# A running sum moved from GpSimd adds to accumulating DMAs, and 16 subtractions moved from GpSimd to VectorE

## The chip, the core and the metric

The kernel runs on one core of one Trainium2 chip. A core has five engines that run their own instruction streams in order and wait for each other through semaphores: TensorE (PE) multiplies matrices, VectorE (DVE) and ScalarE (ACT) work elementwise on SBUF and PSUM, GpSimd (POOL) works elementwise on SBUF, and SyncE (SP) issues DMAs; ACT and POOL issue DMAs too. The metric is the time of one execution on the device, in microseconds (us). A kernel is run several times and the median is given.

## The reference

The model is one layer of a residual block on a sequence of 1024 tokens with 1024 channels, in float32:

```
h = rms_norm(x) * (1 + sc1) + sh1
b, c, v, vc, gl, gates = split(h @ w_in)                    # seven groups of 1024 columns
y_a = (b * causal_dwconv(c * v, 3 taps)) @ w_short_out
u   = causal_dwconv(vc * sigmoid(gl), 31 taps) + bias
y_b = silu(layer_norm(u) over channels) @ w_conf_out
x   = x + g1 * ((sigmoid(ga) * y_a + sigmoid(gb) * y_b) @ w_o)
x   = x + g2 * swiglu_ffn(rms_norm(x) * (1 + sc2) + sh2)
out = rms_norm(x)
```

For the change, two things matter. `q = b * causal_dwconv(c * v, 3 taps)` is the operand of the projection to `y_a`. And LayerNorm needs, for each token, the mean of `u` over all 1024 channels.

## The kernel before

Activations lie with channels on the 128 partitions and tokens along the free dimension, so 1024 channels are eight tiles, numbered j, of 128 x 1024. Every matrix product is made from three fp32r products: an operand is split into a rounded part ("hi", a cast on ScalarE) and the rest ("lo", a subtraction), and PE adds hi·hi, hi·lo and lo·hi in PSUM (lines 283, 284 and 286). Weights are split the same way by `split_w` (lines 205 and 206) as they arrive; up to three blocks are prepared ahead of the one in use.

Most of the input projection, `h @ w_in`, is done by a seven-product scheme on 2 x 2 blocks. There are 12 "duals", each of them two column blocks and seven products, in the order of the string `PRODUCTS`. The weights of a product are sums of weight blocks: GpSimd makes these sums (lines 228 to 232) and the lo parts (line 206) for all 12 duals and for `w_short`; the instructions of its lo parts are collected in `pool_los`. PE results are taken out of PSUM by ScalarE copies and VectorE operations (`win_evac`, lines 551 to 615), which also form `u` before the convolution (kind "u"), the short convolution `sc[j]` (kind "p", line 538) and `q` (kind "q"). `q_store(j)` splits q into hi (ScalarE, line 529) and lo (GpSimd, line 530), and SyncE stores both in DRAM (line 532); `q_load` brings them back while the last dual runs (line 622).

Beside the duals runs the 31-tap convolution, `conv(j)` for the eight channel tiles: 46 VectorE multiply-adds into two PSUM tiles (line 647) for each, then ScalarE writes even and odd tokens back into u's own tile (line 660), and ScalarE's queue stores it as `cv_dram[j]` (line 661). `add_conv(j)` then adds that tile into `tot`, two SBUF tiles of 128 x 512 that hold the running sum over j (line 667). So `tot` ends as the sum over j for each partition; `ln_mean` (line 674) multiplies it with a matrix of ones on PE (line 678), which sums over partitions, and divides on ScalarE (line 679). `ln_square` loads cv back (line 687), subtracts the mean (line 689) and sums squares. All this takes place beside the eight column blocks of `ya`, the product of q with `w_short`; `ln_mean` stands behind the first of them in the program. The next product, `yb`, needs the normalised tiles (`zs`).

The order of the work on each engine is fixed when the kernel is built, by a planner that takes instructions in program order as priority and by its own estimate of when each is ready. `tc.issue_after(ins)` adds that an instruction comes behind `ins` on its engine: the taps are spread over the PSUM reads of the duals in that way, and `add_conv(j)` is put behind a certain weight lo part in GpSimd's queue. An instruction that waits holds up all behind it on its engine. The tiles of u, p, sc, q and the gates share eight buffers (pool "uc"), and the small 128 x 512 tiles share 58 (pool "t").

Of the kernel before, what the change touches and what calls it, by code (L numbers as in the profile page):

```python
# [34 lines left out]
F32 = mybir.dt.float32  # L35
F32R = mybir.dt.float32r
AF = mybir.ActivationFunctionType
ALU = mybir.AluOpType

P = 128  # L40
D = 1024
T = 1024
H = 512
# [64 lines left out]
def block_kernel(ctx: ExitStack, tc: tile.TileContext, x0, xT, c, vecs, ada, w_first, w_plain, w_duals,  # L108
                 w_short, w_conf, w_o, w_fi, w_fo, w_last, outT):
    nc = tc.nc  # L110

    def pool(name, bufs, **kw):
        return ctx.enter_context(tc.tile_pool(name=name, bufs=bufs, **kw))
# [18 lines left out]
    dram = pool("scratch", 1, space=bass.MemoryType.DRAM)  # L132
# [11 lines left out]
    def hl_tile(name, dt=F32R):  # L144
        return tp.tile([P, H], dt, tag="t", name=name)
# [7 lines left out]
    def f32(t):  # L153
        return t.bitcast(F32)

    halves = (slice(0, H), slice(H, T))
# [251 lines left out]
    u = []  # L408
    gate_dram = {(b, j): dram.tile([P, T], F32, name=f"gate_{b}{j}") for b in "ab" for j in range(KC)}

    def uc_tile(name, n=T + CK - 1, dt=F32):
        return ucp.tile([P, T + CK - 1], dt, tag="uc", name=name)[:, :n]
# [24 lines left out]
    for k in range(0, KC, 2):  # L437
        t = uc_tile("x0", T)
# [83 lines left out]
    sc = [None] * KC  # L522
    q_dram = {}

    def q_store(j):

        for h in range(2):
            s = uc_tile("qs", T, F32R)
            nc.scalar.copy(s[:, :H], sc[j][:, halves[h]])
            nc.gpsimd.tensor_tensor(s[:, H:], sc[j][:, halves[h]], f32(s[:, :H]), ALU.subtract)  # L530
            q_dram[j, h] = dram.tile([P, T], F32, name=f"q{j}{h}")
            nc.sync.dma_start(q_dram[j, h], f32(s))

# [17 lines left out]
    def win_evac(pairs):  # L551
# [15 lines left out]
        def evac(i, m, ps):  # L567
# [22 lines left out]
            elif m == "5":  # L590
                e["z"] = e["c"][1] if kind == "g" else g_tile("z")
                nc.scalar.copy(e["z"], ps)
            elif m == "7":
                plus(e["z"], ps, e["z"])
                if kind in "ug":
                    nc.scalar.activation(e["z"], e["z"], AF.Sigmoid, scale=-1.0)
                elif kind == "q":
                    minus_times(sc[j + 1][:, halves[1]], e["z"], sc[j + 1][:, halves[1]])
            else:
                if kind in "ug":  # L600
                    sig = e["c"][0] if kind == "g" else g_tile("sig")
                    nc.scalar.activation(sig, ps, AF.Sigmoid, scale=-1.0)
                if kind == "u":
                    nc.vector.tensor_tensor(e["b"][0], e["b"][0], sig, ALU.mult)
                elif kind == "p":
                    minus_times(e["b"][0], ps, e["b"][0])
                    short_conv(j, e["p"])
                elif kind == "q":
                    minus_times(sc[j + 1][:, halves[0]], ps, sc[j + 1][:, halves[0]])
                    for i in range(2):  # L610
                        q_store(j + i)
                else:
                    for g, t in zip((j, *rest), e["t"]):
                        nc.scalar.dma_start(gate_dram[g], t)
# [17 lines left out]
    def conv(j):  # L632
        eo = u[j].rearrange("p (n two) -> p n two", two=2)
        ev, od = eo[:, :, 0], eo[:, :, 1]
        diff = diffp.tile([P, T + CK - 1], F32, tag="diff", name="diff")
        d, e = diff[:, :NE], diff[:, NE : 2 * NE - 1]
        with tc.issue_after(reads[j * CONV_READS // KC]):
            nc.vector.tensor_tensor(d, ev, od, ALU.subtract)
            nc.vector.tensor_tensor(e, ev[:, 1:], od[:, : NE - 1], ALU.subtract)
        a0, a1 = ps2_tile("c0"), ps2_tile("c1")  # L640
        n = 0

        def tap(out, src, s, wt, acc):
            nonlocal n
            n += 1
            with tc.issue_after(reads[(j * TAPS + n) * CONV_READS // (KC * TAPS)]):
                tap.ins = nc.vector.scalar_tensor_tensor(  # L647
                    out=out, in0=src[:, s : s + H], scalar=wt, in1=acc, op0=ALU.mult, op1=ALU.add
                ).ins

        nc.scalar.activation(a0, od[:, :H], AF.Copy, scale=wsum[:, j : j + 1])
        for s in range(1, CK // 2 + 1):
            last = s == CK // 2
            tap(a0, od, s, col(V_CW + 2 * s * KC, j) if last else wsum[:, s * KC + j : s * KC + j + 1], a0)
        for s in range(CK // 2):
            tap(a1, e, s, col(V_CW + (2 * s + 1) * KC, j), a1 if s else a0)
        for s in range(CK // 2 + 1):
            tap(a0, d, s, col(V_CW + 2 * s * KC, j), a0)
        for i, a in enumerate((a0, a1)):
            nc.scalar.activation(eo[:, : H, i], a, AF.Identity, bias=col(V_CB, j))  # L660
        nc.scalar.dma_start(cv_dram[j], u[j][:, :T])

    def add_conv(j):

        with tc.issue_after(pool_los[(j + 1) * CONV_READS * 7 // (6 * KC) + 5]):
            for h in range(2):
                nc.gpsimd.tensor_tensor(tot[h], tot[h], u[j][:, halves[h]], ALU.add)

    cv = []
    tot = [hl_tile(f"tot{h}", dt=F32) for h in range(2)]  # L670
    for t in tot:
        nc.gpsimd.memset(t, 0.0)

    def ln_mean():
        mu = []
# [57 lines left out]
    for j in range(KC):  # L733
        conv(j)
        add_conv(j)
    ma = {}
    for j in range(KC):
        for h, ps in enumerate(col_block(next_w(), qT, (0, 1), "ya")):
# [424 lines left out]
```

## Time and profile before

| | |
|---|---|
| Median of 3 runs | 1522.57 us (1522.05 to 1522.73) |
| Profiled execution, its own time | 1522.49 us |
| Span of the profiled execution | 1520.7 us |
| Mean granted clock of PE | 0.991 |
| Busy: PE, VectorE, ScalarE, GpSimd | 1474.4, 1179.8, 612.5, 580.9 us |
| Work by GpSimd in line 667 (the sums) | 16 instructions |
| Work by GpSimd in line 530 (q's lo parts) | 16 instructions |

All numbers of the trace come from one execution; its span runs from the first to the last instruction. In the rows of groups, "out<-in" names the tiles written and read, x is the count, then come the busy time in us, the mean of one in ns, and the idle time of the engine just before these instructions with what ended it. In the rows of waits, "A <- B: total, times, longest" says how long A stood still until B released it. Rows of a timeline or of the chain of waits begin with the start and the duration in us. Engine names with a small q are the engine's queue.

### The profile page before, as it was taken

What the parts mean: (1) busy time and instruction counts of PE and PEld (TensorE: products, weight loads), DVE (VectorE), ACT (ScalarE), POOL (GpSimd) and SP (SyncE); (2) the same over time, 40 slices, a digit from 0 to 9 for tenths busy, and PEclk for the clock granted to TensorE, in tenths of its full rate; (3) what the DMA queues carried; (4) which work ended last, traced back from release to release, by engine and by line L of the source; (5) the groups of instructions that cost most, each with busy time, mean ns of one, the idle gap of its engine ahead of it and who ended that gap; (6) DMA issues with size and microseconds to landing.
All of it is one profiled execution on the core that took longest, in us unless ns stands there. A gap on an engine that the chain in (4) does not pass through costs nothing.

```text
span 1520.7 us, 17802 instructions
## 1 busy us (share of the span) xinstructions
PE 1474.4 (97%) x6449; PEld 1202.4 (79%) x6449; DVE 1179.8 (78%) x1566; ACT 612.5 (40%) x871; POOL 580.9 (38%) x483
## 2 busy tenths in 40 slices
PE   6999999999998999999999989999999999999996
PEld 2888887877886888878788868888888888788886
DVE  7997898999997972867777789776666665677756
ACT  4754343443333342335335454444444443211234
POOL 0037788798768883410021001111000016445005
PEclk9999999999999999999999989999999999999998
DMA  9522223232222269655765436554444449998403
GB/s 356 195 63 83 83 70 138 69 111 98 97 84 97 62 223 415 227 180 173 236 203 168 142 103 220 204 171 153 153 152 152 153 153 351 355 299 267 138 15 111
DMA packets 87306, 255.64 MB, mean 168 GB/s; under 512 B 10033, under 2 KB 12209, under 8 KB 87218
## 3 DMA queue, kind: packets, MB, share of 16 engines
q1 hardware_dynamic: 46384, 146.30, 28.7%
q0 software_dynamic: 36944, 95.44, 19.0%
q10 hardware_dynamic: 3890, 12.78, 2.1%
q8 instruction: 50, 0.82, 0.2%
q14 instruction: 38, 0.31, 0.1%
HBM read 187.89 MB, written 66.58 MB: 167 GB/s over the span
## 4 chain that ended last, share of the span: by engine, by line
PE 77%; DVE 10%; DMA 5%; POOL 3%; issue 3%; ACT 1%; SPq 0%; DVEq 0%; ACTq 0%; POOLq 0%
PE x L286 11%; PE x L283 11%; PE x L284 11%; PE z L283 6%; PE z L286 6%; PE z L284 6%; PE y L284 4%; PE y L283 4%; PE y L286 4%; DVE c L647 3%; DMA raw<-in_ada 2%; PE mix L283 2%; PE mix L284 2%; PE mix L286 2%; PE yb L284 2%
## 5 line engine op out<-in xcount | busy, mean ns | idle before, releaser
L205 ACT CAST wh<-raw 128x1024 fp32r<-128x1024 f32 (+2 forms) x257 | 259.0, 1009 | 412.9 <-PE z L284 102.9
L206 POOL TENSOR_TENSOR wl<-raw,wh 128x1024 fp32r<-128x1024 f32 x92 | 237.2, 2586 | 85.5 <-ACT wh L205 85.3
L206 DVE TENSOR_TENSOR wl<-raw,wh 128x1024 fp32r<-128x1024 f32 (+2 forms) x165 | 188.1, 1141 | 50.3 <-ACT wh L205 47.7
L647 DVE SCALAR_TENSOR_TENSOR c<-diff,vec,c 128x512 f32<-128x512 f32 x248 | 182.2, 749 | 6.4 <-DMA q<-qs 2.6
L910 POOL DMA_DIRECT2D hid<-stage x71 | 37.9, 534 | 359.6 <-DVE stage L323 353.3
L284 PE MATMUL x<-tl,wh 128*128 128x512 f32 x336 | 130.7, 389 | 0.0
L283 PE MATMUL x<-th,wh 128*128 128x512 f32 x336 | 130.7, 389 | 0.0
L286 PE MATMUL x<-th,wl 128*128 128x512 f32 x336 | 130.7, 389 | 0.0
L647 DVE SCALAR_TENSOR_TENSOR c<-u,wsum,c 128x512 f32<-128x512 f32 x112 | 84.0, 750 | 1.9
L286 PE MATMUL x<-t2h,wl 128*128 128x512 f32 x184 | 74.2, 404 | 6.2 <-POOL wl L206 5.1
L283 PE MATMUL x<-t2h,wh 128*128 128x512 f32 x184 | 73.5, 401 | 5.5 <-ACT wh L205 2.8
L264 DVE CUSTOM_DVE_ANT_0 raw<-raw,cs,vec 128x1024 f32<-128x1024 f32 x24 | 34.5, 1441 | 52.2 <-DMA raw<-in_ada 41.0
L283 PEld LDWEIGHTS x<-th,wh 128*128 128x128 f32 x336 | 63.1, 188 | 13.1 <-issue 0.2
L284 PE MATMUL x<-t2l,wh 128*128 128x512 f32 x184 | 73.3, 399 | 0.1
L284 PEld LDWEIGHTS x<-tl,wh 128*128 128x128 f32 x336 | 63.1, 188 | 13.1
L286 PEld LDWEIGHTS x<-th,wl 128*128 128x128 f32 x336 | 63.1, 188 | 13.1
L283 PE MATMUL z<-th,wh 128*128 128x512 f32 x168 | 65.4, 390 | 1.6 <-ACT wh L205 1.6
L228 POOL TENSOR_TENSOR raw<-raw 128x1024 f32<-128x1024 f32 x12 | 29.2, 2436 | 98.6 <-DVE wl L206 94.0
L286 PE MATMUL z<-th,wl 128*128 128x512 f32 x168 | 65.5, 390 | 0.0
L284 PE MATMUL z<-tl,wh 128*128 128x512 f32 x168 | 65.4, 389 | 0.0
L322 ACT CAST stage<-g 128x512 fp32r<-128x512 f32 x62 | 38.3, 621 | 55.7 <-DMA hid<-stage 27.8
L323 DVE TENSOR_TENSOR stage<-g,stage 128x512 fp32r<-128x512 f32 x62 | 42.4, 687 | 22.8 <-ACT stage L322 22.6
(797 smaller groups left out, 4081.6 us busy)
## 6 DMA issues: line engine op xcount, KB each, us to landing
hid<-stage POOLq DMA_DIRECT2D x71, 512.0 KB, 4.2
raw<-in_w_fi SPq DMA_DIRECT2D x50, 512.0 KB, 4.4
raw<-in_w_duals SPq DMA_DIRECT2D x48, 512.0 KB, 3.5
th<-hid POOLq DMA_DIRECT2D x71, 256.0 KB, 5.7
tl<-hid POOLq DMA_DIRECT2D x71, 256.0 KB, 6.2
ada<-in_ada SPq DMA_DIRECT2D x24, 512.0 KB, 6.2
raw<-in_ada SPq DMA_DIRECT2D x24, 512.0 KB, 4.6
raw<-in_w_fo SPq DMA_DIRECT2D x24, 384.0 KB, 5.9
```

The lines of the kernel that those rows point to most:

```text
L205: nc.scalar.copy(wh, raw)
L206: lo = lo_engine.tensor_tensor(wl, raw, f32(wh), ALU.subtract)
L228: eng.tensor_tensor(a["s1"], a["21"], a["22"], ALU.add)
L264: nc.vector.tensor_tensor_reduce(out=raw, in0=raw, in1=cs, scale=1.0, scalar=col(V_ADA, b), op0=ALU.mult, op1=ALU.add, accum_out=modc(b),)
L283: nc.tensor.matmul(ps, wh, xh, start=first, stop=False, skip_group_check=again)
L284: nc.tensor.matmul(ps, wh, xl, start=False, stop=False, skip_group_check=again)
L286: mm3.ins = nc.tensor.matmul(ps, wl, xh, start=False, stop=last, skip_group_check=again).ins
L322: nc.scalar.copy(hi, src)
L323: nc.vector.tensor_tensor(lo, src, f32(hi), ALU.subtract)
L647: tap.ins = nc.vector.scalar_tensor_tensor(out=out, in0=src[:, s : s + H], scalar=wt, in1=acc, op0=ALU.mult, op1=ALU.add).ins
L910: nc.gpsimd.dma_start(hid_dram[key], s)
```

## The change

Two things move off GpSimd's arithmetic. First, q's lo parts (line 530) are made by VectorE instead of GpSimd. Second, the running sum no longer lies in SBUF: `tot_dram` is a DRAM tile of 128 x 1024, and `add_conv(j)` issues one DMA from GpSimd's queue that stores u's tile there for j = 0 and adds it to what is there for the others, at the same place in GpSimd's order as the two adds before. The two SBUF tiles `tot` are allocated after the last `add_conv` and loaded from `tot_dram` by two DMAs, also from GpSimd's queue; the two memsets go. `ln_mean` is as before.

```diff
@@ -527,7 +527,7 @@
         for h in range(2):
             s = uc_tile("qs", T, F32R)
             nc.scalar.copy(s[:, :H], sc[j][:, halves[h]])
-            nc.gpsimd.tensor_tensor(s[:, H:], sc[j][:, halves[h]], f32(s[:, :H]), ALU.subtract)
+            nc.vector.tensor_tensor(s[:, H:], sc[j][:, halves[h]], f32(s[:, :H]), ALU.subtract)
             q_dram[j, h] = dram.tile([P, T], F32, name=f"q{j}{h}")
             nc.sync.dma_start(q_dram[j, h], f32(s))
 
@@ -663,13 +663,10 @@
     def add_conv(j):
 
         with tc.issue_after(pool_los[(j + 1) * CONV_READS * 7 // (6 * KC) + 5]):
-            for h in range(2):
-                nc.gpsimd.tensor_tensor(tot[h], tot[h], u[j][:, halves[h]], ALU.add)
+            nc.gpsimd.dma_start(tot_dram, u[j][:, :T], **({"accum_op": ALU.add} if j else {}))
 
     cv = []
-    tot = [hl_tile(f"tot{h}", dt=F32) for h in range(2)]
-    for t in tot:
-        nc.gpsimd.memset(t, 0.0)
+    tot_dram = dram.tile([P, T], F32, name="tot")
 
     def ln_mean():
         mu = []
@@ -733,6 +730,9 @@
     for j in range(KC):
         conv(j)
         add_conv(j)
+    tot = [hl_tile(f"tot{h}", dt=F32) for h in range(2)]
+    for t, s in zip(tot, halves):
+        nc.gpsimd.dma_start(t, tot_dram[:, s])
     ma = {}
     for j in range(KC):
         for h, ps in enumerate(col_block(next_w(), qT, (0, 1), "ya")):
```

## The prediction

> **What bounds the kernel now.** I read the page first, then the waits of PE, then the busy table by stretches.
>
> ```profile
> span 1520.7 us, 17802 instructions
> PE 1474.4 (97%) x6449; PEld 1202.4 (79%) x6449; DVE 1179.8 (78%) x1566; ACT 612.5 (40%) x871; POOL 580.9 (38%) x483
> ```
>
> PE is busy for 97% of the span, so a change pays only where it removes idle or slow PE time. POOL's 38% is an average that hides the stage in question, from about 96 to 584 us, where the seven-product input projection runs beside the convolution. There PE waited for this:
>
> ```profile
> PE x L286 <- POOL wl L206: 8.8, 5, 3.5
> PE x L283 <- ACT u L577: 0.4, 1, 0.4
> PE y L286 <- POOL wl L206: 0.4, 1, 0.4
> ```
>
> These are the waits of PE between 200 and 560 us (total, times, longest). Of 9.6 us, 9.2 are for POOL's low part of a weight block; none is for VectorE. The table by stretches (columns PE, PEld, DVE, ACT, POOL busy with instruction counts, PE clock, DMA share, GB/s) shows where:
>
> ```profile
> 290.00:310.00 20.00, 18.85 (x83) 15.28 (x83) 19.82 (x27) 8.12 (x10) 17.20 (x8) 1.00 0.23 80
> 350.00:370.00 20.00, 18.57 (x82) 15.04 (x81) 19.29 (x27) 8.93 (x13) 15.35 (x9) 1.00 0.48 159
> 410.00:430.00 20.00, 20.00 (x90) 16.57 (x89) 19.86 (x23) 7.45 (x9) 19.42 (x8) 1.00 0.03 2
> 450.00:470.00 20.00, 17.08 (x75) 13.52 (x74) 16.12 (x23) 8.00 (x11) 19.53 (x10) 1.00 0.13 53
> 470.00:490.00 20.00, 16.52 (x65) 13.13 (x65) 19.73 (x27) 4.35 (x6) 16.10 (x7) 0.91 0.41 131
> 200.00:560.00 360.00, 350.40 (x1527) 286.70 (x1527) 337.47 (x437) 134.49 (x183) 295.55 (x130) 1.00 0.30 100
> ```
>
> A full stretch holds 90 matmuls, 0.222 us each (third row). The other four 20 us rows hold 83, 82, 75 and 65: 55 missing, 55 x 0.222 = 12.2 us of PE. That is more than the waits, because PE comes back slow after the longest one: the granted clock of that stretch is 0.91, and the chain of waits shows matmuls of double length there.
>
> ```profile
> 479.55 0.24 PE x L283
> ...
> 480.40 0.43 PE x L283
> ```
>
> What POOL did before the waits, in order of time (start, duration):
>
> ```profile
> 292.56 3.47 POOL L667 TENSOR_TENSOR tot<-tot,u 128x512 f32<-128x512 f32 x2 [3.50 <-ACT u L660]
> ...
> 352.07 3.00 POOL L530 TENSOR_TENSOR qs<-sc,qs 128x512 fp32r<-128x512 f32 x2
> ...
> 452.68 1.75 POOL L667 TENSOR_TENSOR tot<-tot,u 128x512 f32<-128x512 f32 x1
> ...
> 456.75 1.29 POOL L667 TENSOR_TENSOR tot<-tot,u 128x512 f32<-128x512 f32 x1
> ...
> 466.10 1.30 POOL L530 TENSOR_TENSOR qs<-sc,qs 128x512 fp32r<-128x512 f32 x1
> ...
> 472.20 4.48 POOL L530 TENSOR_TENSOR qs<-sc,qs 128x512 fp32r<-128x512 f32 x2
> 476.65 7.03 POOL L206 TENSOR_TENSOR wl<-raw,wh 128x1024 fp32r<-128x1024 f32 x3
> ```
>
> The two sums (3.0 us) and three lo parts of q (5.8 us), 8.8 us together, stand ahead of the weight lo that PE waits for at 479. The change moves exactly these.
>
> **The change part by part.**
>
> ```profile
> L206 POOL TENSOR_TENSOR wl<-raw,wh 128x1024 fp32r<-128x1024 f32 x92 | 237.2, 2586 | 85.5 <-ACT wh L205 85.3
> L667 POOL TENSOR_TENSOR tot<-tot,u 128x512 f32<-128x512 f32 x16 | 23.7, 1497 | 3.5 <-ACT u L660 3.5
> L530 POOL TENSOR_TENSOR qs<-sc,qs 128x512 fp32r<-128x512 f32 x16 | 23.5, 1480 | 8.4 <-ACT qs L529 8.4
> L910 POOL DMA_DIRECT2D hid<-stage x71 | 37.9, 534 | 359.6 <-DVE stage L323 353.3
> ```
>
> 1. *Off POOL.* 16 sums (23.7 us) and 16 lo parts (23.5 us) leave: 47.2 us. Eight accumulating issues of 512 KB and two loads come in. No accumulating DMA is in the trace; the nearest row is a plain 512 KB store from POOL, 0.534 us of POOL each. From below, 10 x 0.53 = 5.3 us; from above, the 23.7 us of the adds they replace (3.0 us an issue). I take 0.53, the same instruction on the same queue. POOL then carries about 42 us less, and the 8.8 us in front of the long wait become 0.5. The two waits together cost 40 missing matmuls, 8.9 us, of which some 1.7 is the slow clock after the second, which goes with it. In the rows of 290 and 350 PE lost 7 and 8 matmuls, 1.6 and 1.8 us, behind 3.5 us of sums and 3.0 us of lo parts. I credit the whole **12.2 us**. From below it is 0, if the weights' hi casts on ScalarE, which POOL also waits for, set the same instants.
>
> 2. *Onto VectorE.* 16 subtractions of 128x512, in order among the evacuations and the taps.
>
> ```profile
> L323 DVE TENSOR_TENSOR stage<-g,stage 128x512 fp32r<-128x512 f32 x62 | 42.4, 687 | 22.8 <-ACT stage L322 22.6
> L323 DVE TENSOR_TENSOR tl<-x,th 128x512 fp32r<-128x512 f32 x11 | 17.8, 1664 | 2.3 <-ACT th L322 2.2
> L538 DVE SCALAR_TENSOR_TENSOR sc<-p,vec,sc 128x1024 f32<-128x1024 f32 x12 | 33.0, 2752 | 1.3 <-ACT sc L536 1.3
> L587 DVE TENSOR_TENSOR sc<-v,sc 128x512 f32<-128x512 f32 x4 | 3.0, 754 | 0.0
> ```
>
> The same operation takes 0.687 us late in the kernel, where POOL is idle, and 1.664 us in the first part of this stage, where POOL reads SBUF. So 11.0 to 26.6 us. I take 1.1 us each, 17.6 us, since the multiplication that makes its operand (L587, last row, 0.754 us) is near the lower end while L538 shows stretching. VectorE was busy 337.5 of 360 us between 200 and 560, and these waits fall away or shrink, because they were for the very work that leaves POOL:
>
> ```profile
> DVE u L416 <- POOL qs L530: 5.1, 1, 5.1
> DVE c L647 <- DMA q<-qs: 2.6, 1, 2.6
> DVE p L561 <- POOL qs L530: 1.3, 1, 1.3
> ```
>
> That is 9.0 us of its 22.5 idle. New need 337.5 + 17.6 = 355 us against 360 - 12.2 = 348. Less POOL traffic shortens the stretched operations a little (13% fewer POOL microseconds; L538, twice as wide, would take 1.37 us by the first row, so it alone is stretched by 12 x 1.38 = 17 us), some 3 to 5 us. VectorE thus falls about 3 us behind over the stage, and behind each lo part, which waits for ScalarE's cast, stand evacuations that PE's banks wait for. Part hides behind the taps' tail (point 4): **+2 us**; ends 0 and 26.6 - 9.0 = 17.6, near the lower since PE never waited for VectorE here.
>
> The weighing of a rule: by the Trainium skill, "SBUF — State Buffer", Who interferes with whom, a VectorE instruction with two SBUF inputs contends with a GpSimd instruction that reads SBUF, through an exclusive lock; the 1.664 against 0.687 us agrees. If each of the 16 met a whole POOL split (2.586 us, row above), 16 x (0.687 + 2.586) = 52 us is the estimate, and VectorE would rule the stage, beyond the rival D below.
>
> 3. *The sums in DRAM, all but the last.* They are issued where the adds were, and each waits in POOL's queue for ScalarE's conv output, as the add did (3.5 us once, row above), and for the previous accumulate, some 57 us old (the convs end at 163.7 to 560.1, row in point 4, eight of them). Behind it stand the weight lo parts. As it starts no earlier than the add and holds POOL 2.5 us less, it costs nothing; cover gone (a conv later than POOL), it costs that lag. The uc buffer of u is now released by the DMA's end; a plain 512 KB store of the same tile lands in 2.6 us (row below), the two adds took 3.0.
>
> 4. *The last sum and the way back.* Before, the last adds stood between splits at 568; now a DMA, then two loads waiting for it in POOL's queue ahead of further weight splits, then the mean's matmul.
>
> ```profile
> L660 ACT ACTIVATE u<-c,vec x16: 714/722/732, 163.7 to 560.1; 128x512 f32<-128x512 f32 x16
> 568.03 2.55 POOL L667 TENSOR_TENSOR tot<-tot,u 128x512 f32<-128x512 f32 x2
> 594.58 1.88 PE L678 MATMUL mu<-tot,ones 128*128 128x512 f32 x4
> 560.00:607.00 47.00, 47.00 (x206) 38.20 (x205) 8.58 (x15) 15.12 (x22) 21.20 (x11) 1.00 1.03 404
> cv<-u ACTq DMA_DIRECT2D x8, 512.0 KB, 2.6
> x<-x_dram POOLq DMA_DIRECT2D x8, 512.0 KB, 8.3
> 597.99 8.83 DMA cv<-cv
> 606.95 3.01 DVE cv L689 x5
> PE yb L284 <- DVE zsl L315: 0.3, 1, 0.3
> ```
>
> The last conv ends at 560.8, set by VectorE, not PE. PE, 12.2 us ahead, asks for the sum at 594.6 - 12.2 = 582.4. Between lie 21.6 us for accumulate and load. The load: 8.3 us (POOL's 512 KB from DRAM). The accumulate: no row; 2.6 us from below, from above twice the 8.8 us that a transfer takes in the crowded 560 to 607 us (share 1.03). Sum 10.9 to 25.9 us with the load; nearer the lower, since it starts as the crowd forms: no wait of PE, but little margin. The subtraction L689 waits for cv's load at 607 anyway. What does cost is the bytes: DMA is full there at 404 GB/s, and 0.52 MB accumulated plus 0.52 MB loaded are 2.6 us more (0 if they fill gaps; 5.2 if the accumulate also moves the old sum both ways). The LayerNorm path runs behind these loads, and PE starts yb with 0.3 us of waiting, so no slack: **+2.6 us**.
>
> A second sentence from the Trainium skill, "Collectives: The Full Stack", The bandwidth ceiling: a DMA that adds reads two sources for one write. No run here shows it; by it the accumulate would be nearer 5.2 than 2.6.
>
> 5. *Removed besides:* two memsets on POOL ahead of the stage, and two SBUF tiles held from there on; no wait of the trace names them as its end.
>
> Sum against the profiled run (1522.49 us, its span 1520.7 and 1.8 around; the median is 1522.57): 1522.5 - 12.2 + 2.0 + 2.6 = **1514.9 us**.
>
> **The rivals.**
> - *B, VectorE takes most back.* For it: the 99% VectorE load of 410 to 430 in the table. Against: no PE wait for it. With 9 us of lag instead of 2: 1521.9 at worst with the tail, about 1519 with a hidden tail.
> - *C, the stalls only change their owner.* PE's waits for wl become waits for wh or for u L577, ScalarE standing in order behind the taps. For it: POOL idled 85.5 us for ScalarE's casts. Against: POOL ran without a break before 479. Time 1522.5.
> - *D, slower, by VectorE.* The lo parts meet POOL at every turn and wait for the cast with evacuations behind them. It decides once the added VectorE time passes 9.0 + 12.2 = 21.2 us, 1.33 us a piece with nothing hidden; with 26.6 and 0.2 us of cast wait a piece it is 29.8 - 21.2 = 8.6 over, 1531.
> - *E, slower, by the sum's way.* PE stands at L678 in order once accumulate and load pass 21.6 us, and the gain is gone at 21.6 + 12.2 - 4.6 = 29 us; at 38 us, 1531.
>
> **How the numbers follow.** 0.2% is 3.0 us, about what a measurement can tell. The forecast with its own range 1508 to 1518.5: 0.57. B (to 1519.5): 0.13. C: 0.07. D 0.13, E 0.10. Faster 0.70, same 0.07, slower 0.23. The range runs from 1508 (full credit with a hidden tail, and nearly 2 us from the small losses I left out) to 1528, into D and E; beyond it lie some 0.17.
>
> **What the new profile would show.** Right: no PE wait for wl between 200 and 560, 90 matmuls in the stretches above, POOL near 255 us there and the mean's matmul near 582. Point 2: the new VectorE group near 1.1 us. Point 4: yb waiting for zsl about 3 us. Wrong: PE waiting for VectorE or for ScalarE behind it in the stage (B, C, D), or at mu (E); also an accumulate that holds POOL over 3 us.

## The result

The changed kernel takes 1531.12 us (1529.75 to 1533.56), against 1522.31 us before: a ratio of 1.0069 (95% interval 1.0052 to 1.0086), slower by 0.7%. The forecast was 1514.9 us, with 1508 to 1528 as its range. The time that came out is the one that rival D gave (1531, by VectorE).

The first rows of the page after (the profiled execution itself took 1532.48 us):

```profile
span 1530.7 us, 17786 instructions
PE 1477.8 (97%) x6449; PEld 1203.7 (79%) x6449; DVE 1208.4 (79%) x1582; ACT 610.9 (40%) x871; POOL 541.9 (35%) x459
```

POOL lost 39 us of work and VectorE gained 29. The groups of instructions of the touched lines after (count, busy us, mean ns, idle before them):

```profile
L206 POOL TENSOR_TENSOR wl<-raw,wh 128x1024 fp32r<-128x1024 f32 x92 | 238.7, 2607 | 142.4 <-ACT wh L205 138.3 <-PE z L284 4.0
L530 DVE TENSOR_TENSOR qs<-sc,qs 128x512 fp32r<-128x512 f32 x16 | 21.9, 1387 | 0.0
L666 POOL DMA_DIRECT2D tot<-u x8 | 6.9, 864 | 8.5 <-ACT u L660 4.8 <-PE x L284 3.7
L735 POOL DMA_DIRECT2D tot<-tot x2 | 1.1, 574 | 2.8 <-DMA tot<-u 2.8
```

The lo parts cost VectorE 21.9 us, with no idle time in front of them: they never waited for ScalarE's cast. Before, POOL's weight lo parts stood 85.3 us in wait of ScalarE's hi casts, now 138.3: POOL is no longer late. The waits of PE between 200 and 560 us say the same, and who is late instead:

```profile
PE x L283 <- DVE z L545: 5.6, 2, 4.4
PE x L286 <- POOL wl L206: 1.8, 3, 0.8
PE x L283 <- ACT v L577: 1.2, 1, 1.2
PE x L283 <- ACT sig L577: 1.1, 1, 1.1
PE x L283 <- DVE sig L545: 0.7, 2, 0.4
PE x L283 <- ACT p L577: 0.5, 1, 0.5
```

POOL's share fell from 9.2 to 1.8 us, and 9.1 us for VectorE and ScalarE took its place. The busy table by stretches (PE, PEld, DVE, ACT, POOL, each with its count; PE clock, DMA share, GB/s), first in the stage, then behind it:

```profile
450.00:470.00 20.00, 15.64 (x57) 12.39 (x56) 19.86 (x19) 3.35 (x4) 11.54 (x6) 0.83 0.24 54
470.00:490.00 20.00, 20.00 (x90) 16.57 (x89) 19.87 (x26) 8.92 (x12) 14.95 (x6) 1.00 0.49 164
200.00:560.00 360.00, 349.08 (x1516) 285.25 (x1515) 354.01 (x442) 131.49 (x182) 259.89 (x108) 0.99 0.34 107
...
560.00:570.00 10.00, 10.00 (x45) 7.98 (x43) 9.68 (x14) 2.06 (x3) 2.99 (x2) 1.00 1.00 333
570.00:580.00 10.00, 8.12 (x37) 6.69 (x37) 1.52 (x3) 6.06 (x10) 6.39 (x4) 1.00 1.06 344
580.00:590.00 10.00, 8.54 (x38) 6.75 (x36) 1.38 (x2) 0.63 (x1) 1.14 (x2) 1.00 1.02 388
590.00:600.00 10.00, 7.24 (x18) 5.29 (x19) 2.72 (x1) 4.54 (x6) 7.04 (x3) 0.66 1.02 405
```

The stretch of 470, where PE had 65 matmuls, is full with 90, but 450 fell from 75 to 57. Over the 360 us there are 1516 matmuls instead of 1527, 11 fewer, 2.4 us. The larger loss in this trace lies behind the stage. The rows of 570 to 600 hold 37, 38 and 18 matmuls; before, the same three held these:

```profile
570.00:580.00 10.00, 10.00 (x46) 8.29 (x45) 2.77 (x4) 2.86 (x4) 5.33 (x3) 1.00 1.05 406
580.00:590.00 10.00, 10.00 (x46) 8.29 (x45) 0.00 (x0) 2.85 (x5) 2.40 (x1) 1.00 1.04 415
590.00:600.00 10.00, 10.00 (x42) 7.56 (x42) 1.90 (x3) 3.12 (x4) 6.73 (x4) 1.00 1.03 421
```

That is 134 against 93, 41 x 0.222 = 9.1 us. With the 2.4 it makes 11.5, of which the rest of the kernel gives about 1.5 back; the spans differ by 10.0 us.

Two things fail there. First, VectorE is 97% busy up to 570 us, where it had 0.69 us of work in that row before, because the last convolution ends later:

```profile
L660 ACT ACTIVATE u<-c,vec x16: 708/721/730, 163.5 to 570.2; 128x512 f32<-128x512 f32 x16
```

It was at 560.1 before. Second, a load has changed its place on SyncE's queue. Before, the first block of `w_short` was asked for ahead of q's loads; after, behind the last of them. The timeline of SyncE's queue, before and then after (start, duration):

```profile
556.30 0.33 SPq L191 DMA_DIRECT2D raw<-in_w_short  x1
556.75 0.36 SPq L622 DMA_DIRECT2D q00h<-q  x1
```

```profile
582.32 0.32 SPq L622 DMA_DIRECT2D q71l<-q  x1
582.96 1.63 SPq L191 DMA_DIRECT2D raw<-in_w_short  x3
...
591.28 1.04 ACT L205 CAST wh<-raw 128x1024 fp32r<-128x1024 f32 x1 [9.51 <-DMA raw<-in_w_short]
...
592.38 0.79 PE L283 MATMUL ya<-q00h,wh 128*128 128x512 f32 x1 [3.84 <-ACT wh L205]
```

ScalarE stood 9.5 us for that block and PE 3.8 us behind it, and came back at a slow clock (0.66 in the stretch of 590). The planner made this order when the kernel was built, by its own estimates of when each instruction is ready. Among the kernels below, the load stands this late in those that have all 16 lo parts and all taps on VectorE (lo_only, after_p6), unless it is traced ahead (after_short).

### The profile page after: what moved, and what is told of

Same layout as the page of the kernel before. It is cut to its first block, busy times and chain, and to the rows that moved or that the text cites. A ratio compares the mean times of both kernels' runs of the same rounds, so it can differ in the third digit from the quotient of the medians.

```text
span 1530.7 us, 17786 instructions
## 1 busy us (share of the span) xinstructions
PE 1477.8 (97%) x6449; PEld 1203.7 (79%) x6449; DVE 1208.4 (79%) x1582; ACT 610.9 (40%) x871; POOL 541.9 (35%) x459
## 4 chain that ended last, share of the span: by engine, by line
PE 58%; DVE 2%; DMA 1%; issue 1%; ACT 0%; POOL 0%; DVEq 0%; ACTq 0%; SPq 0%; POOLq 0%
PE x L286 7%; PE x L283 7%; PE x L284 7%; PE z L283 4%; PE z L284 4%; PE z L286 4%; PE y L284 3%; PE y L283 3%; PE y L286 3%; PE ya L286 2%; PE ya L283 2%; PE ya L284 2%; PE mix L286 2%; PE mix L283 2%; PE mix L284 2%; PE yb L283 2%
## 5 line engine op out<-in xcount | busy, mean ns | idle before, releaser
L206 POOL TENSOR_TENSOR wl<-raw,wh 128x1024 fp32r<-128x1024 f32 x92 | 238.7, 2607 | 142.4 <-ACT wh L205 138.3
```

The source lines that it names most:

```text
L206: lo = lo_engine.tensor_tensor(wl, raw, f32(wh), ALU.subtract)
```

## The experiments

Each kernel is timed beside the kernel before on the same chip; the ratio is to that. "Before" took 1518.97 to 1520.96 us in these sets and 1522.31 in the first, so differences of a few microseconds between sets are read from the ratios. The first four expectations speak of a Theory 1 (T1 below), which is that the lo parts overfill VectorE; against it stand the sum's way through DRAM and the order of loads. "Matmuls" and "VectorE" are the count of PE and the busy time of VectorE in the 200 to 560 us row; "conv" is the start of the last conv output (L660 or its equal).

| Kernel | us | ratio (95%) | matmuls | VectorE | conv |
|---|---|---|---|---|---|
| before | 1522.3 | 1 | 1527 | 337.5 | 560.1 |
| changed | 1531.1 | 1.0069 (1.0052, 1.0086) | 1516 | 354.0 | 570.2 |
| dma_only | 1527.8 | 1.0050 (1.0035, 1.0066) | 1509 | 343.3 | 563.0 |
| dma_p6 | 1519.1 | 0.9991 (0.9981, 1.0002) | 1544 | 335.8 | 555.6 |
| dma_p4 | 1521.2 | 1.0014 (1.0005, 1.0024) | 1529 | 339.3 | 558.8 |
| lo_only | 1526.9 | 1.0048 (1.0031, 1.0066) | 1530 | 353.9 | 567.1 |
| after_short | 1528.8 | 1.0058 (1.0037, 1.0079) | 1518 | 354.0 | 570.1 |
| after_p6 | 1530.5 | 1.0077 (1.0056, 1.0099) | 1523 | 354.0 | 569.2 |
| after_taps | 1520.1 | 0.9998 (0.9989, 1.0008) | 1542 | 345.4 | 558.5 |
| before_taps | 1522.7 | 1.0018 (1.0007, 1.0030) | 1517 | 319.2 | 560.9 |
| no_lo | 1509.7 | 0.9932 (0.9915, 0.9949) | 1578 | 340.1 | 546.8 |
| no_sum | 1514.3 | 0.9958 (0.9943, 0.9973) | 1555 | 334.3 | 552.6 |
| lo_half | 1514.3 | 0.9959 (0.9945, 0.9974) | 1551 | 348.8 | 556.6 |
| lo_half0 | 1511.0 | 0.9938 (0.9918, 0.9957) | 1568 | 347.1 | 555.0 |
| half_dma | 1518.9 | 0.9998 (0.9988, 1.0007) | 1548 | 351.9 | 558.4 |
| half_dma6 | 1518.9 | 0.9994 (0.9985, 1.0004) | 1545 | 353.0 | 560.4 |
| late_split | 1522.8 | 1.0013 (1.0002, 1.0025) | 1563 | 345.9 | 555.2 |
| late_dma | 1532.0 | 1.0068 (1.0049, 1.0086) | 1555 | 351.8 | 554.7 |
| late_two | 1514.8 | 0.9969 (0.9957, 0.9981) | 1566 | 343.3 | 553.1 |
| late_two_dma | 1514.8 | 0.9966 (0.9956, 0.9976) | 1587 | 348.2 | 547.8 |

### Each half of the change alone

The sum alone in DRAM (dma_only: the changed kernel with the lo parts back on GpSimd), and the lo parts alone on VectorE (lo_only: the kernel before with this line):

```diff
-            nc.gpsimd.tensor_tensor(s[:, H:], sc[j][:, halves[h]], f32(s[:, :H]), ALU.subtract)
+            nc.vector.tensor_tensor(s[:, H:], sc[j][:, halves[h]], f32(s[:, :H]), ALU.subtract)
```

> The sums by accumulating DMAs, q's lo parts back on GpSimd. Theory 1 (VectorE's added lo parts are what costs): no PE wait for VectorE or ScalarE worth over 2 us between 200 and 560 us, some of the waits for the weights' lo parts left, the first w_short load ahead of q's loads again and no stop of PE before ya; 1515 to 1520 us. Rival (the sum's way through DRAM costs, by its issues on GpSimd or its bytes beside q's loads): 1527 us or more.

> q's lo parts on VectorE, the sums added on GpSimd as before the change. Theory 1: PE waits for VectorE and for ScalarE behind it as in the changed kernel, and stops before ya for the first w_short block; 1528 to 1536 us. Rival (the sum's way costs): 1520 us or less.

Both lose by about half a per cent: 1.0050 and 1.0048. dma_only took the rival's time, lo_only 1526.9, just under T1's range. Together they lose hardly more (1.0069), so the losses do not add. In lo_only PE keeps its matmuls in the stage (1530) and loses behind it (568 between 560 and 700 us, where the kernel before has 609), as in the changed kernel: it too has a late conv, and the same order of loads. In dma_only most of the loss is in the stage: 1509 matmuls, 18 fewer than before, 4.0 us. The trace shows its largest single piece. The timeline of dma_only on POOL and VectorE:

```profile
352.50 2.80 POOL L530 TENSOR_TENSOR qs<-sc,qs 128x512 fp32r<-128x512 f32 x2
355.03 7.31 POOL L206 TENSOR_TENSOR wl<-raw,wh 128x1024 fp32r<-128x1024 f32 x3
...
354.33 8.56 DVE L604 TENSOR_TENSOR u<-u,sig 128x512 f32<-128x512 f32 x1
```

And the wait of PE behind it, from the waits between 360 and 380 us:

```profile
PE x L283 <- ACT p L577: 4.5, 1, 4.5
```

One VectorE multiplication of two SBUF operands lasted 8.56 us, from the second of GpSimd's five instructions here to half a microsecond past the last of them; ScalarE stood behind VectorE, and PE behind ScalarE. The changed kernel has such an operation at another place, behind its long wait in the stretch of 450:

```profile
453.14 0.87 POOL L666 DMA_DIRECT2D tot<-u  x1
453.68 5.61 DVE L639 TENSOR_TENSOR diff<-u 128x526 f32<-128x526 f32 x1
453.75 2.67 POOL L229 TENSOR_TENSOR raw<-raw 128x1024 f32<-128x1024 f32 x1
456.10 2.62 POOL L206 TENSOR_TENSOR wl<-raw,wh 128x1024 fp32r<-128x1024 f32 x1
...
459.21 0.68 DVE L545 TENSOR_TENSOR z<-x,z 128x512 f32<-128x512 f32 x1
...
459.95 0.80 PE L283 MATMUL x<-th,wh 128*128 128x512 f32 x1 [4.36 <-DVE z L545]
```

The row of 453.68 begins while GpSimd issues the DMA of line 666 (453.14 to 454.01). That is no single case. Between 90 and 575 us, none of the eight kernels here without a sum in DRAM has a VectorE operation of over 3.6 us. Nine of the twelve that have it show one or two, 13 together, and 11 of these begin during such an issue; that of 8.56 us is one of the two that do not. So most of these long operations come with the moment at which a DMA of the sum is issued. lo_only has none, and its loss has another cause.

### The order of the first w_short load

after_short is the changed kernel with that one load traced ahead of q's loads:

```diff
+    short_0 = []
+    plan += [lambda: split_w(short_0[0], 1024, (), nc.gpsimd)]
-    plan += [(w_short[k], 1024, (), nc.gpsimd) for k in range(KC)]
+    plan += [(w_short[k], 1024, (), nc.gpsimd) for k in range(1, KC)]
...
             if d == n_duals - 1:
+                if i == 0:
+                    short_0.append(load(w_short[0]))
```

> The changed kernel with the first w_short block's load issued ahead of q's loads (in the changed kernel it stands behind the last of them). Theory 1: the stop of PE at 588 to 599 us (3.8 + 0.4 us of waits and some 3 us of slow clock) goes, the waits for VectorE stay: 1523 to 1526 us. Rival (the stop is there because DMA is full, whatever the order): 1530 to 1532 us with the same stop.

The stop before `ya` is gone, and T1's 1523 to 1526 us are missed. Between 560 and 700 us PE has 585 matmuls against 569, 3.6 us; the medians differ by 2.3 us and the ratios by 1.7, and the intervals overlap. The stage is as it was without this edit (1518 matmuls, conv at 570.1). The order of loads is at most a small part of the loss.

### No lo parts, no sum

no_lo is the changed kernel without q's lo subtraction (only the hi halves are stored, and both loads read them); no_sum is the kernel before with `add_conv` empty.

```diff
-            nc.vector.tensor_tensor(s[:, H:], sc[j][:, halves[h]], f32(s[:, :H]), ALU.subtract)
```

```diff
-        with tc.issue_after(pool_los[(j + 1) * CONV_READS * 7 // (6 * KC) + 5]):
-            for h in range(2):
-                nc.gpsimd.tensor_tensor(tot[h], tot[h], u[j][:, halves[h]], ALU.add)
+        return
```

> The changed kernel without q's lo parts on any engine: only the hi half is stored, and both loads read it, so that the second operand of the ya products is the hi part again and not the lo part. Theory 1: with GpSimd relieved and VectorE not loaded, PE between 200 and 560 us loses under 4 us instead of 16.6, and the w_short load is ahead again: 1510 to 1515 us. Rival (the sum's way costs): 1525 us or more.

> The kernel before without the running sum: add_conv does nothing, tot stays zero, so the mean that LayerNorm takes off is left out (sixteen additions of 2.0 to 2.4 us on GpSimd, of which eight pairs fall before the last conv's end). Lo parts stay on GpSimd. It carries the removal of GpSimd's work that the two halves of the change share, and no accumulating DMA. If the accumulating DMAs themselves cost the 7.5 us that the run with the sum alone in DRAM lost, this one gains against before: 1508 to 1515 us. If the loss comes from GpSimd's remaining work falling at other times against VectorE (VectorE held 5 to 9 us at once, PE stopping behind it), it stays at or above before: 1517 to 1527 us, with at least one VectorE operation of over 5 us in 100 to 560 us.

The row of no_lo by stretches:

```profile
200.00:560.00 360.00, 358.17 (x1578) 295.42 (x1577) 340.13 (x440) 140.79 (x193) 270.17 (x112) 1.00 0.36 114
```

With the lo parts off POOL and on no other engine, PE has 51 matmuls more than before, nearly all of the 55 that the prediction counted as missing. So GpSimd's work is worth what it was taken for, if no other engine pays for it. Without a sum the gain is 0.42%. Between no_lo and the changed kernel lies the subtraction on VectorE, with the stores of its results: by the ratios (1.0069 less 0.9932) some 21 us. Neither of these runs says yet why the sum in DRAM loses.

### The sum's place in GpSimd's order

dma_p6 and dma_p4 are dma_only with the accumulating DMA one w lo part later and one earlier:

```diff
-        with tc.issue_after(pool_los[(j + 1) * CONV_READS * 7 // (6 * KC) + 5]):
+        with tc.issue_after(pool_los[(j + 1) * CONV_READS * 7 // (6 * KC) + 6]):
```

> The sum alone in DRAM, lo parts on GpSimd, each accumulating DMA issued one w lo part later in GpSimd's order. Same work, same DMAs, other times. If the loss of the run with the sum alone in DRAM (1527.8) is a cost of its DMAs, it stays: 1525 to 1530 us. If it is a matter of where GpSimd's instructions meet VectorE's, the long VectorE operations (8.56 us at 354) go to other places or vanish, and the time moves by some us either way: 1515 to 1524 us if the one at 354 goes and none replaces it.

> The sum alone in DRAM, lo parts on GpSimd, each accumulating DMA one w lo part earlier than in the change instead of later. Theory: the place in GpSimd's order sets where instructions meet, so a third place gives a third time, with no trend from early to late: anywhere in 1512 to 1530 us, above 1524 only with a VectorE operation of over 5 us that ScalarE and then PE stand behind. Rival: the earlier an accumulating DMA, the worse (it holds GpSimd for its tap): 1530 us or more, beyond the 1527.8 of the change's own place.

Same work and same DMAs at three places: 1521.2, 1527.8 and 1519.1 us. The middle one, the change's own, is the worst, so it is no matter of earlier or later. The operation that lasted 8.56 us in dma_only is this one in dma_p6:

```profile
350.91 1.12 DVE L604 TENSOR_TENSOR u<-u,sig 128x512 f32<-128x512 f32 x1
```

dma_p4 has an operation of 6.90 us at 341 (`diff<-u`), behind which PE did not stand, and its time is near that of the kernel before. dma_p4 has 20 matmuls more in the stage than dma_only, 4.4 us, which is about the one wait of 4.5 us. So such an operation costs where PE is due behind it, and the same DMAs at another place do not lose dma_only's half per cent. But none of the three places gains what no_sum does.

after_p6 makes the same step in the changed kernel.

> The changed kernel with each accumulating DMA one w lo part later in GpSimd's order; lo parts stay on VectorE. Theory: the sum's move costs by where GpSimd's remaining work meets VectorE's (alone, that one step took it from 1527.8 to 1519.1), the lo parts by VectorE's load. Then what is left here is the cost of the lo parts alone, with fewer long VectorE operations: 1522 to 1528 us, and the 5.6 us operations at 184 and 454 us are gone. Rival: with VectorE 97% busy in 200 to 560 us, it is full whatever the meetings, and the order on GpSimd does not matter: 1529 to 1533 us, as the changed kernel.

It took the rival's time, 1530.5 us. The 5.6 us operations at 184 and 454 are gone, and nothing is won in time. In the stage PE has 7 matmuls more (1523) and still waits 4.3 us for VectorE's z, in four pieces. Behind it the stop for the first `w_short` block has grown from 3.8 to 6.9 us, and from 560 to 700 us there are 555 matmuls instead of 569 (this profiled execution, 1534.85 us, is the slowest of the four). So the loss remains without any operation of over 3.6 us, with VectorE at 354 us; that such operations cost nothing here is not shown.

### Is it VectorE's load?

after_taps and before_taps leave out 4 of the 46 taps of each convolution, 24 us of VectorE, in the changed kernel and in the kernel before. The lo parts stay where each kernel has them.

```diff
             nonlocal n
             n += 1
+            if n % 11 == 10:
+                return
```

> The changed kernel with 4 of the 46 taps of each convolution left out (32 instructions of 0.75 us on VectorE, 24 us, of which 21 fall in 200 to 560 us; so u is not the reference's convolution). The lo parts stay on VectorE, at their places. Theory: the change lost because 21.9 us more of VectorE's time do not fit beside PE, and the time they cost comes back whatever work of VectorE's is taken away: the last conv ends before 561 us and the time is 1510 to 1521 us. Rival: it is the place of the lo parts (behind a cast of ScalarE's, ahead of evacuations) or the sum's way through DRAM: then the time stays at 1525 us or more.

> The kernel before with the same 4 taps of each convolution left out. It shows what VectorE's time alone is worth with the lo parts on GpSimd. If VectorE was already half of what bounds the stage, it gains, though POOL's weight lo parts still make PE wait: 1510 to 1518 us. If only POOL bounded it (as the prediction read the waits), it stays at 1518 to 1523 us.

In the changed kernel 11 us come back, although the lo parts stand on VectorE as they did. In the kernel before, the same 24 us gain nothing (1.0018): there, VectorE was not what PE waited for. The stage's row of after_taps, and the first two of PE's waits there:

```profile
200.00:560.00 360.00, 353.03 (x1542) 288.01 (x1542) 345.37 (x428) 134.44 (x185) 266.36 (x108) 1.00 0.36 115
```

```profile
PE x L286 <- POOL wl L206: 2.3, 5, 0.8
PE z L283 <- ACT sig L592: 1.7, 1, 1.7
```

VectorE has 14.6 us of idle time again and PE waits for no one long. The last conv ends at 558.5. One thing is mixed in: the first `w_short` load is back ahead of q's loads here too, which after_short puts at some 2 us. The other 9 us point to VectorE's load; that the lo parts' places or the sum's way hold the time at 1525 or more, the rival, is excluded.

### Half of the lo parts

lo_half and lo_half0 are the kernel before with 8 of the 16 lo parts on VectorE, those of the second or of the first halves (the second is shown):

```diff
-            nc.gpsimd.tensor_tensor(s[:, H:], sc[j][:, halves[h]], f32(s[:, :H]), ALU.subtract)
+            (nc.vector if h else nc.gpsimd).tensor_tensor(s[:, H:], sc[j][:, halves[h]], f32(s[:, :H]), ALU.subtract)
```

> The kernel before with 8 of the 16 lo parts on VectorE (one half of each pair), sums as adds on GpSimd. All 16 cost 8 us. If VectorE has a threshold (about 11 us of idle time that was left in the stage), 8 parts at 1.39 us, 11 us, cost little: 1517 to 1523 us, perhaps less, as GpSimd loses 12 us. If each part costs alike, half: 1522 to 1525 us.

> The kernel before with the other 8 of the 16 lo parts on VectorE, those of the first halves; sums as adds on GpSimd. Same work on each engine as in the first half split (1514.3), another order. If that gain is one of load (GpSimd 12 us lighter, VectorE still below its limit), it comes again: 1512 to 1517 us. If it was luck of the order, as with the sum at three places, anywhere up to 1522 us.

Half of the move gains 0.4 and 0.6% where the whole loses 0.5%, more than the ranges of both expectations. lo_half0 is the fastest kernel here that computes all: 1510.96 us, 0.9938 (0.9918 to 0.9957). Its row of the stage, then the waits of PE there, then its two groups of lo parts:

```profile
200.00:560.00 360.00, 356.70 (x1568) 293.74 (x1567) 347.05 (x446) 140.61 (x192) 293.46 (x124) 1.00 0.32 109
```

```profile
PE x L286 <- POOL wl L206: 2.7, 3, 1.6
PE x L283 <- DVE sig L545: 0.4, 1, 0.4
PE y L286 <- POOL wl L206: 0.2, 1, 0.2
```

```profile
L530 DVE TENSOR_TENSOR qs<-sc,qs 128x512 fp32r<-128x512 f32 x8 | 12.6, 1575 | 0.1
L530 POOL TENSOR_TENSOR qs<-sc,qs 128x512 fp32r<-128x512 f32 x8 | 11.8, 1474 | 6.2 <-ACT qs L529 6.2
```

A lo part on VectorE is dearer here (1.575 us) than in the changed kernel (1.387), and still the kernel gains: the price of one does not decide, the sum against VectorE's room does. With 12.6 us more VectorE stays at 347 us; with 21.9 it is at 354.

half_dma and half_dma6 put the sum in DRAM on top of lo_half, at the change's own place and one later.

> The changed kernel with 8 of its 16 lo parts back on GpSimd: the sum in DRAM at the change's own place, half of the lo parts on VectorE. If the threshold in VectorE's time is the whole of the loss, it is at the half split's time (1514.3) or below it, as GpSimd loses another 23.7 us: 1508 to 1515 us. If the sum's move at this place costs by itself (alone it stood at 1527.8, with VectorE held 8.6 us), it is above: 1518 to 1526 us.

> The same with each accumulating DMA one w lo part later in GpSimd's order (alone there 1519.1). If the place matters by what it makes meet, the two kernels of this pair differ by several us, and the one without VectorE operations of over 5 us is the faster: this one 1510 to 1517 us.

Both give back what the half split won, 1518.9 us each, and do not differ by several us, as was expected of the pair. So the sum in DRAM costs 4.6 us here against lo_half (5 to 6 by the ratios), at both places. The stage is not where it is lost: the counts there are 1548 and 1545 against 1551. It is lost behind it. The rows of 560 to 700 us of lo_half and then of half_dma, and a wait of PE there in half_dma:

```profile
560.00:700.00 140.00, 140.00 (x612) 114.55 (x611) 87.15 (x121) 54.47 (x74) 36.97 (x32) 1.00 0.71 260
560.00:700.00 140.00, 136.77 (x595) 111.20 (x594) 83.18 (x120) 54.23 (x76) 40.77 (x34) 1.00 0.72 263
```

```profile
PE yb L283 <- DVE ma L742: 3.0, 1, 3.0
```

17 matmuls are 3.8 us. `ma` takes the last blocks of `ya` out of PSUM, and VectorE does it in order among its work for LayerNorm, which the sum and the loads of cv feed. This wait is in those kernels with the sum in DRAM that split q ahead of its store, unless PE stopped for the `w_short` block before: 0.9 us in dma_only, 1.4 in after_short, 1.6 in no_lo, 1.7 in dma_p6, 2.3 in dma_p4, 3.0 and 3.1 in this pair, 3.7 in after_taps. No kernel that adds on GpSimd has it. No run takes apart whether the sum's bytes or the new order of instructions brings it about.

### Another place for the split

late_split stores q unsplit and splits it after its load, in the stretch behind the stage; late_dma has the sum in DRAM besides. late_two issues all sixteen loads first and splits in a loop of its own; late_two_dma has the sum in DRAM too, one place later. The core of late_split, and of late_two against late_split:

```diff
-            s = uc_tile("qs", T, F32R)
-            nc.scalar.copy(s[:, :H], sc[j][:, halves[h]])
-            nc.gpsimd.tensor_tensor(s[:, H:], sc[j][:, halves[h]], f32(s[:, :H]), ALU.subtract)
-            q_dram[j, h] = dram.tile([P, T], F32, name=f"q{j}{h}")
-            nc.sync.dma_start(q_dram[j, h], f32(s))
+            q_dram[j, h] = dram.tile([P, H], F32, name=f"q{j}{h}")
+            nc.sync.dma_start(q_dram[j, h], sc[j][:, halves[h]])
...
-        for t, s in zip(qT[j][h], halves):
-            nc.sync.dma_start(f32(t), q_dram[j, h][:, s])
+        hi, lo = qT[j][h]
+        nc.sync.dma_start(f32(lo), q_dram[j, h])
+        t_split(f32(lo), hi, lo)
```

```diff
-        t_split(f32(lo), hi, lo)
...
+    for j in range(KC):
+        for h in range(2):
+            hi, lo = qT[j][h]
+            t_split(f32(lo), hi, lo)
     for j in range(KC):
         conv(j)
```

> The kernel before with q stored unsplit (half the bytes) and split after its load, in the stretch after 560 us: the hi copies leave ScalarE's and the lo subtractions GpSimd's queue in 200 to 560 us, and VectorE does them after the last conv, where it is idle most of the time. The sums stay additions on GpSimd. If the stage's loss is shared work on GpSimd and VectorE, it gains like the run without lo parts or somewhat less, as GpSimd keeps the additions (47 us): 1509 to 1516 us. If the split after the load is late for q's first matmuls, PE waits in 570 to 620 us and it gives the gain back: 1518 to 1524 us.

> The same late split with the sum in DRAM. If halves add where neither puts work on VectorE in 200 to 560 us: 1505 to 1511 us, at or below the run without lo parts (1509.7). If moving the sum into DRAM costs here too what it cost alone (7.5 us), it stands that much above the late split with additions: 1517 to 1523 us.

> The late split with all sixteen loads of q issued ahead of the loads that stood between them, the splits in a loop of their own behind them; the sums are additions on GpSimd. The first late split lost 12.1 us of PE's time in 560 to 700 us (2.6 before) waiting for q's parts. If that came from the loads' order, 8 to 9 us of it return: 1512 to 1516 us. If the splits themselves are late on ScalarE or VectorE: 1518 to 1523 us, with PE still waiting for a q part after 585 us.

> The same with the sum in DRAM, at the later place in GpSimd's order. By the runs so far the sum's move at that place is worth between nothing and the 6 us of the kernel without a sum: 1506 to 1516 us. If long VectorE operations come back and PE stands behind them, 1518 to 1526 us.

In late_split the stage is good (1563 matmuls), and the gain is lost behind it, because q's loads stand between other loads on SyncE's queue. A wait of PE between 560 and 620 us:

```profile
PE ya L283 <- ACT q50h L322: 5.5, 1, 5.5
```

late_two, with the loads in front, has no such wait, and 8 us come back (7 by the ratios): 0.9969. With the sum in DRAM the pair gives 1.0068 and 0.9966. In the second (one place later) it costs nothing. In the first (the change's own place) it costs 9 us, more than either branch of its expectation had. Little of that is in the stage (1555 matmuls against 1563): behind it, from 560 to 700 us, there are 524 against 562, and PE waits 11.7 us for parts of q instead of 6.6. So these 9 us are mainly the late loads of q once more.

## Why the prediction was wrong

**Point 1, off POOL: right in what it is worth, wrong in that PE would get it.** POOL came to 259.9 us where 255 was forecast, and PE's waits for it fell from 9.2 to 1.8 us. The credit of 12.2 us is there when no other engine pays (no_lo: 51 matmuls, 11.3 us). In the changed kernel the count of the stage fell by 11 instead. The lower bound that was named, 0, by ScalarE's hi casts, was not how it went: POOL's longer idle time before them is slack.

**Point 2, onto VectorE: this is the step that failed.** The lo parts measured 1.387 us each, 21.9 us, not 1.1 and 17.6; still inside its bounds. The 9.0 us of waits did fall away: of VectorE's own waits in the stage 1.2 us are left. What failed is the last line, "+2 us", with its reason that PE never waited for VectorE. VectorE had 22.5 us of idle time in 360 and was asked for 21.9, and 16.5 of them show as busy time (354.0 against 337.5); the rest is a later end. The loss at the end of the stage and behind it is about 9 us (conv at 570.2, 41 matmuls), of which 2 to 4 belong to the order of loads (after_short), and the credit is gone as well; against no_lo the term of +2 is some 21 us. The half split, after_taps and before_taps show that this is a limit of load. Rival D had the mechanism and its condition right (over 21.2 us added, over 1.33 us a piece). That it named 1531 is luck: its sum took 1.664 us a piece and a cast wait of 0.2 us. There is no idle time before L530, and with the measured 21.9 us the same sum gives 0.7 us over, 1523.

On the rule weighed there: by the Trainium skill, "SBUF — State Buffer", Who interferes with whom, a VectorE instruction with two SBUF inputs contends with a GpSimd instruction that reads SBUF. The estimate for 16 whole meetings was 52 us; the group measured 21.9, about 0.7 us of meeting a piece over the 0.687 us that it takes undisturbed. The contention is there, but it falls unevenly: the median of the 16 is 0.780 us, the longest 2.909.

**Point 3, the sums in DRAM: "costs nothing" was wrong as a whole, right in its parts.** An issue held POOL 0.864 us, between 0.53 and 3.0 and nearer the lower, which was taken. POOL waited 8.5 us in front of the eight, more than the 3.5 before. But the sum in DRAM is not free: set against adds it cost between nothing and 9 us, by the kernel and by its place. Two steps were not seen. Each place of the issues in GpSimd's order sets anew which of VectorE's operations are held long, and whether PE stands behind them; this fits dma_only against dma_p4 and dma_p6. And VectorE's work for LayerNorm comes later, so that PE waits at yb (0.9 to 3.7 us). dma_p6 against no_sum (1519.1 and 1514.3 us) has 7 matmuls fewer from 560 to 700 us, where that wait is, and 11 fewer in the stage; what costs these 11 stays open.

**Point 4, the last sum: right that PE does not wait for it; what it cost shows only where PE is on time.** The last accumulate left at 575.2 and the loads at 581.4; the mean's matmul ran at 606.9 without a wait, so rival E fell. The accumulates' time to landing, from the rows of line 666, and the matmul, from those of the tile `tot`:

```profile
DMA to landing us min/median/max: 3.1/6.0/7.0
```

```profile
L675 PE MATMUL mu<-tot,ones x4: 591/592/592, 606.9 to 608.2; 128*128 128x512 f32 x4
```

The +2.6 us do not show in the changed kernel: it has no wait for `zsl` any more, against 0.3 us. PE comes to yb late there. Where it comes on time it waits for `ma` instead, 0.9 to 3.1 us with all taps, so the term was near in size, on another wait than the one named; that bytes are its cause is not shown. By the Trainium skill, "Collectives: The Full Stack", The bandwidth ceiling, an add needs two source reads. The landings agree: the first of the eight, a plain store, landed after 3.1 us, the seven adds after 5.4 to 7.0, far below the 17.6 us that point 4 allowed. What point 4 missed is on the same queue as q's loads: the first `w_short` block, issued at 583.0 instead of 556.3. It cost some 2 us by after_short, within the noise.

**Point 5, the two tiles: said to cost nothing.** They did move something: with `tot` out of SBUF, the planner puts q's first two loads into the stage, at 224.7 us (they stood at 556.8 before). No run takes this apart from the sum's way; allocating `tot` early as before, with the sum in DRAM, wasn't tried. It is one of the things that could make up what is open.

```profile
224.73 0.33 SPq L622 DMA_DIRECT2D q00h<-q  x1
225.10 0.42 SPq L622 DMA_DIRECT2D q00l<-q  x1
```

**The rivals.** B had the mechanism and too small a size. C was partly right: the stalls of the stage changed owner, to VectorE first and to ScalarE behind it. The chance of 0.23 for slower was too low, because the prediction left two engines near full and credited one of them as if the other had room.

## What to carry to other kernels

Where two engines beside PE are both nearly full in a stage (here VectorE 94% and GpSimd 82%), set the moved work, at the duration it has on its new engine while the other one works, against that engine's idle time in that stage, and do not count all of that time as free: of 22.5 us idle, 12.0 and 12.6 us of lo parts gained 0.4 to 0.6%, and 21.9 us lost 0.5%. Look at the end of the stage too, since an engine that lags there makes PE pay after it, and see whether a planner has put a load at another place. Before a gain or a loss of a few microseconds is put down to an edit of one engine's order, run it at a second and third place: here the same DMAs gave 1519, 1521 and 1528 us.

## What was not expected of the hardware

- A VectorE operation with two SBUF inputs was held through several GpSimd instructions in a row, not one: 8.56 us until the last of five had ended, against 1.12 us for the same line in dma_p6, and 5.61 us over two. Of 13 such operations in 20 kernels, 11 begin while GpSimd issues a DMA. By the Trainium skill, "SBUF — State Buffer", Who interferes with whom, the order of issue decides which of the two is blocked, by an exclusive lock; the traces agree that VectorE is held, but for longer than one instruction, and in the row of 5.61 us the record of VectorE's operation starts 0.07 us ahead of GpSimd's.
- An accumulating DMA of 512 KB into DRAM, issued by GpSimd, held it 0.86 to 0.91 us and landed after 5.4 to 7.0 us. The plain store of the same size on the same queue, the first of the eight, held it 0.72 us and landed after 3.1. The count of bytes on the profile's page (before, then after) rose by 4.2 MB written, which is eight tiles, and by only 0.52 MB read, which is the load of `tot`: the seven reads of the old sum are not in it.

```profile
HBM read 187.89 MB, written 66.58 MB: 167 GB/s over the span
HBM read 188.41 MB, written 70.78 MB: 169 GB/s over the span
```
